# Reading turned attention probabilities back from the DRAM scratch in two halves instead of one transfer

## The chip, the core and the metric

The kernel runs on one core of one Trainium2 chip. The metric is the device time of one launch in microseconds (us). A lower number is better.

## What is computed

The reference is one decoder block over 512 positions with 1024 channels (the Griffin-style merge of a gated short convolution and of native sparse attention, then a feed-forward part with a short convolution). Cut to what matters here:

```python
proj = rmsnorm(x, norm1_g) @ w_in            # split into a_b, a_c, a_x, q, k/v of three branches, gates
y_a = a_b * causal_dwconv(a_c * a_x, conv_a_w)
# per head group g and block of 128 queries, for the selected and for the window branch:
s = einsum('bqghd,bkgd->bghqk', qc, k) * scale
p = masked_softmax(s, mask)                  # over the keys
o = einsum('bghqk,bkgd->bqghd', p, v)
y_b = gate0 * o_cmp + gate1 * o_sel + gate2 * o_win
mix = sigmoid(gA) * (y_a @ w_a_out) + sigmoid(gB) * (y_b @ w_b_out)
x = x + mix @ w_o
x = x + (silu(causal_dwconv(g) + b) * u) @ w_ffn_out      # g, u = split(rmsnorm(x) @ w_ffn_in)
```

With 512 positions and 8 key blocks of 64 all blocks are selected, so that both the selected and the window branch see every key up to the query.

## The kernel before

Matrix products are computed from pairs of values, a rounded part and its remainder (`h` and `l` in names), so that each product of two tiles takes three matmuls. All matmuls run on TensorE (PE). In order of time: the token-wise projections, then (from about 98 us to 295 us) the attention, then the output projection and the feed-forward part.

**Attention.** `attend` (line 609) is called for each tile of 128 queries, `qt` = 3, 2, 1, 0, and each of two head groups `g`. A tile `qt` sees `qt + 1` tiles of 128 keys. For `qt` > 0 each call makes two steps, one for the window branch (`br` = 1) and one for the selected branch (`br` = 0); for `qt` = 0 both branches make one step. I call such a step a *turn*, since its centre is the function `turn` (line 624): turn 1 is `qt` 3, `g` 0, `br` 1; turn 2 is `br` 0 of it; turns 3 and 4 are the same with `g` 1; turns 5 to 8 belong to `qt` 2, 9 to 12 to `qt` 1, 13 and 14 to `qt` 0. There are fourteen, and only turns 1 to 4 have four key tiles.

One turn goes like this. PE makes the scores of four heads into PSUM banks (lines 640 and 641). VectorE (DVE) adds the causal mask and takes the maximum (692, 693). ScalarE (ACT) takes the exponentials (694) and scales them by the sums and gates (700). The probabilities then lie with queries on the partitions, while the product with the values needs keys there. `turn` does that in three parts: DVE transposes in blocks of 32 by 32 (627); four transfers on SyncE's queue (SP) write the blocks to a scratch in DRAM (633); one transfer reads them back with the keys on the partitions, into a tile `tn` (635). Per key tile `kt`, ACT copies the rounded part `ph` (724), GpSimd (POOL) subtracts it from `tn` to leave the remainder (725), and PE multiplies both by the values into the bank `po` (727 and 732). Of `ph` there are two buffers (`NPT`), and of `tn` two (`NTN`), so that the read-back of a turn waits until PE has used up the turn two before it.

**What lies beside it.** The products of the short convolution (`pa`, line 762) and of the merge gates (`pg`, 783; `pma`, 796) don't depend on the attention and fill PE between its steps. Each takes a weight tile: loaded on SP into one of three `wr` buffers (139), rounded by ACT (143), and its remainder taken by POOL (145; in conv tiles partly by a DMA). A weight load can be issued only when POOL has finished with the tile three loads earlier. All of these stand in SP's one queue together with the turns' transfers.

**What sets the order.** Nothing is ordered by hand around the change. The program is built with a scheduler (`schedule_with_timeline_sim=True`, line 1143), which places the instructions of every engine by its own estimates of their times. Each engine then works through its list in order on the chip, waiting where a semaphore isn't there yet.

Of the kernel before, what the change touches and what calls it, by code (L numbers as in the profile page):

```python
# [22 lines left out]
NT = S // P  # L23
# [30 lines left out]
QB = P // SQ  # L54
# [31 lines left out]
def tile_block(ctx: ExitStack, tc: tile.TileContext, xT, pos, par, par2, w_tok, w_a3, w_gate, w_ao, w_bo, w_o,  # L86
               w_ff, w_dn, c_w1, out):
    nc = tc.nc
# [90 lines left out]
    def ring_w(src, name):  # L179
        raw = raw_tile(name)  # L180
        nc.sync.dma_start(raw, src)
        h, l = ring(name)
        split(h, l, raw)
        return h, l
# [424 lines left out]
    def attend(pt_, g, qt):  # L609
# [14 lines left out]
        def turn(e, n):  # L624

            v = e.rearrange("p b k h i -> p (b k h i)")
            nc.vector.transpose(v, v)
            w = n * P
            dst = pt_.tile([P, HG * S], F32R, name=f"tn_{e.name}", tag="tn", bufs=NTN)[:, 0:QB * w]
            d = dst.bitcast(F32)  # L630
            mid = dr.tile([QB, QB, SQ, w], F32, name=f"td_{e.name}", tag=f"td_{e.name}", bufs=1)
            for a in range(QB):
                nc.sync.dma_start(mid[a].rearrange("b j r -> j b r"),
                                  v[a * SQ:(a + 1) * SQ].rearrange("p (b r) -> p b r", b=QB))
            nc.sync.dma_start(d.rearrange("p (a r) -> p a r", a=QB), mid.rearrange("a b j r -> (b j) a r"))
            return dst.rearrange("p (a k r) -> p a k r", a=QB, k=n)

        def scores(w, i, br, a, b):
# [18 lines left out]
        if qt == 0:  # L657

            e = e_tile("", 2)
            mx = pt_.tile([P, HG, 2], F32, name=f"mx{tag}", tag="mx", bufs=1)  # L660
            sums = small("sums", 2)
            for i in range(HG):
                sc = s_bank(f"sc{tag}{i}")
                w = sc[:, 0:2 * (NC + P)].rearrange("p (b k) -> p b k", b=2)
                for j in range(2):
                    nc.tensor.matmul(w, q[:, g * HG + i, :], kk5[:, j, :, g, 0:NC + P], start=j == 0, stop=j == 1)
                nc.vector.tensor_add(xc[:, i, :], w[:, 0, 0:NC], cm_add[:, qt, :])
                dg = w[:, :, NC:]
                nc.vector.tensor_tensor(dg, dg, causal[:, None, :].to_broadcast([P, 2, P]), op=ALU.add)
                nc.vector.tensor_reduce(mx[:, i], dg, axis=AX.X, op=ALU.max, negate=True)  # L670
                for br in (1, 0):
                    nc.scalar.activation(e[:, :, br, i], dg[:, br].rearrange("p (b i) -> p b i", i=SQ), AF.Exp,
                                         bias=mx[:, i, br:br + 1], accum_out=sums[:, i, br:br + 1])
            nc.vector.reciprocal(sums, sums)
            nc.gpsimd.tensor_mul(sums, sums, gates[:, :, 1:3])
            for br in (1, 0):
                nc.vector.tensor_tensor(e[:, :, br], e[:, :, br],
                                        sums[:, None, :, br:br + 1].to_broadcast([P, QB, HG, SQ]), op=ALU.mult)
            turned = turn(e, 2)
        for br in (1, 0):  # L680
            if qt > 0:
                o = off if br == 0 else 0
                e = e_tile(br, qt + 1)
                mx = small(f"mx{br}", 1)
                sums = small(f"sums{br}", 1)
                for i in range(HG):
                    sc = s_bank(f"sc{tag}{i}{br}")
                    scores(sc[:, 0:o + nk], i, br, NC - o, NC + nk)
                    if o:
                        nc.vector.tensor_add(xc[:, i, :], sc[:, 0:NC], cm_add[:, qt, :])  # L690
                    dg = sc[:, o + nk - P:o + nk]
                    nc.vector.tensor_add(dg, dg, causal)
                    nc.vector.tensor_reduce(mx[:, i], sc[:, o:o + nk], axis=AX.X, op=ALU.max, negate=True)
                    nc.scalar.activation(e[:, :, :, i].rearrange("p b k i -> p k b i"),
                                         sc[:, o:o + nk].rearrange("p (k b i) -> p k b i", b=QB, i=SQ), AF.Exp,
                                         bias=mx[:, i], accum_out=sums[:, i])
                scale_of(sums, 1 + br)
                for i in range(HG):
                    v = e[:, :, :, i]
                    nc.scalar.activation(v, v, AF.Copy, scale=sums[:, i])  # L700
                turned = turn(e, qt + 1)
# [18 lines left out]
            for kt in range(qt + 1):  # L720
# [5 lines left out]
                w = v_t[:, kt, 2 * br + g, :]  # L726
# [116 lines left out]
    for i in range(4):  # L843
# [3 lines left out]
        w = ring_w(w_bo[i], f"bo{i}")  # L847
# [33 lines left out]
    for n, j in enumerate(O_ORDER):  # L881
        w = ring_w(w_o[j], f"o{j}")
# [265 lines left out]
```

## Time and profile before

| what | before |
|---|---|
| time, median of 3 runs | 700.33 us (699.7 to 702.07) |
| the profiled execution | 700.2 us, of which span 698.5 us |
| PE busy | 690.7 us (99% of the span) |
| ACT, DVE, POOL busy | 436.8, 508.3, 242.6 us |
| DMA, mean over the span | 179 GB/s |
| HBM read, written | 111.55 MB, 12.58 MB |

The profiled execution is 0.13 us below the median. The span is the time from its first to its last instruction; 1.7 us lie around it. Matmuls are pipelined: one of 512 columns is listed with about 0.39 us, but in an unbroken row the next one starts 0.227 us after it. So a wait of PE is read from the distance between starts.

### The profile page before, as it was taken

The numbers are of one execution on the slowest core, as the hardware profiler recorded it, in microseconds if no ns is written. First come the engines' busy times: TensorE is split into PE (matmuls) and PEld (weight loads), VectorE is DVE, ScalarE is ACT, GpSimd is POOL, SyncE is SP. The second block draws the span as 40 slices with busy tenths as digits, with TensorE's granted clock in tenths as the row PEclk, the third lists the DMA queues.
The fourth block names the chain that finished last, engine by engine and source line by source line (L and its number), as shares of the span: only waits on it lengthen the run. The fifth ranks groups of instructions, "written<-read, shape, count | busy, mean of one in ns | idle before, by whom it ended". The sixth has DMA issues, their size and how long they took to land.

```text
span 698.5 us, 11286 instructions
## 1 busy us (share of the span) xinstructions
PE 690.7 (99%) x4125; PEld 616.7 (88%) x4125; DVE 508.3 (73%) x886; ACT 436.8 (63%) x775; POOL 242.6 (35%) x240
## 2 busy tenths in 40 slices
PE   9999999999999999999999999999999999999997
PEld 8999878887888888888889999999999999999986
DVE  6886885766576646475887899988787777877543
ACT  7634654777897877534685777766466665556530
POOL 3060423476887867452011212121112221112110
PEclk9999999999999999999999999999999999999999
DMA  7333586577676555563486797997977879775675
GB/s 272 108 96 122 156 184 143 139 254 216 230 232 224 164 174 148 186 237 117 135 194 127 196 230 175 239 201 183 228 180 167 210 178 221 180 177 108 129 141 150
DMA packets 56167, 124.87 MB, mean 179 GB/s; under 512 B 5040, under 2 KB 20528, under 8 KB 56112
## 3 DMA queue, kind: packets, MB, share of 16 engines
q1 hardware_dynamic: 41984, 91.39, 40.8%
q0 software_dynamic: 13840, 32.51, 27.1%
q8 instruction: 32, 0.52, 0.3%
q10 hardware_dynamic: 288, 0.26, 0.1%
q14 instruction: 23, 0.19, 0.1%
HBM read 111.55 MB, written 12.58 MB: 178 GB/s over the span
## 4 chain that ended last, share of the span: by engine, by line
PE 89%; DMA 5%; ACT 2%; DVE 1%; issue 1%; SPq 0%; ACTq 0%
PE p L418 10%; PE p L417 10%; PE p L420 10%; PE pdn L418 6%; PE pdn L417 6%; PE pdn L420 6%; PE pg L417 4%; PE pg L418 4%; PE pg L420 4%; PE po L418 2%; PE po L417 2%; PE po L420 2%; DMA tn_e<-td_e 2%; PE pa L417 2%; PE pa L418 2%; PE pj_s L264 2%
## 5 line engine op out<-in xcount | busy, mean ns | idle before, releaser
L418 PE MATMUL p<-xf_l,sh 128*128 128x256 f32 x336 | 80.6, 277 | 0.0
L417 PE MATMUL p<-xf_h,sh 128*128 128x256 f32 x336 | 80.5, 277 | 0.0
L170 POOL DMA_DIRECT2D wl_s<-in_w_ff_dram x22 | 19.4, 883 | 167.2 <-ACT wl_s L169 146.4
L162 ACT ACTIVATE sh<-s 128x1024 fp32r<-128x1024 f32 x44 | 46.2, 1057 | 37.4 <-PE p L418 24.7
L418 PE MATMUL pdn<-al,wh_d 128*128 128x512 f32 x176 | 68.7, 391 | 0.0
L417 PE MATMUL pdn<-ah,wh_d 128*128 128x512 f32 x176 | 68.5, 390 | 0.0
L417 PEld LDWEIGHTS p<-xf_h,sh 128*128 128x128 f32 x336 | 63.0, 188 | 0.1
L418 PEld LDWEIGHTS p<-xf_l,sh 128*128 128x128 f32 x336 | 63.0, 188 | 0.1
L163 DVE TENSOR_TENSOR sl<-s,sh 128x1024 fp32r<-128x1024 f32 x44 | 53.6, 1220 | 8.7 <-ACT sh L162 8.7
L725 POOL TENSOR_TENSOR tn_e<-tn_e,ph 128x512 fp32r<-128x512 f32 x40 | 51.2, 1296 | 16.0 <-ACT ph L724 15.9
L168 ACT ACTIVATE wh_s<-wr_s 128x1024 fp32r<-128x1024 f32 x22 | 23.3, 1059 | 53.3 <-PE pdn L418 50.1
L170 POOL DMA_DIRECT2D wl_d<-in_w_dn_dram x22 | 26.4, 1199 | 76.5 <-ACT wl_d L169 69.2
L420 PE MATMUL p<-xf_h,sl 128*128 128x256 f32 x336 | 51.5, 277 | 0.0
L417 PE MATMUL pg<-xg_h,wh_g 128*128 128x512 f32 x128 | 50.1, 392 | 0.0
L418 PE MATMUL pg<-xg_l,wh_g 128*128 128x512 f32 x128 | 50.1, 392 | 0.0
L420 PE MATMUL pdn<-ah,wl_d 128*128 128x512 f32 x176 | 47.7, 389 | 0.0
L420 PEld LDWEIGHTS p<-xf_h,sl 128*128 128x128 f32 x336 | 44.5, 188 | 0.2
L1067 DVE TENSOR_TENSOR x<-x,pdn 128x512 f32<-128x512 f32 x48 | 32.9, 685 | 16.2 <-PE pdn L420 15.5
L145 POOL TENSOR_TENSOR wl_g<-wr_g,wh_g 128x1024 fp32r<-128x1024 f32 x16 | 38.5, 2408 | 10.0 <-ACT wh_g L143 9.7
L417 PE MATMUL p<-xf_h,wh_s 128*128 128x256 f32 x168 | 40.5, 276 | 0.0
L418 PE MATMUL p<-xf_l,wh_s 128*128 128x256 f32 x168 | 40.5, 276 | 0.0
L420 PEld LDWEIGHTS pdn<-ah,wl_d 128*128 128x128 f32 x176 | 33.0, 188 | 6.9
(358 smaller groups left out, 2095.6 us busy)
## 6 DMA issues: line engine op xcount, KB each, us to landing
wr_s<-in_w_ff_dram SPq DMA_DIRECT2D x44, 512.0 KB, 5.2
wl_s<-in_w_ff_dram POOLq DMA_DIRECT2D x22, 512.0 KB, 7.5
wr_d<-in_w_dn_dram SPq DMA_DIRECT2D x22, 512.0 KB, 6.8
wl_d<-in_w_dn_dram POOLq DMA_DIRECT2D x22, 512.0 KB, 8.7
wr_g<-in_w_gate_dram SPq DMA_DIRECT2D x16, 512.0 KB, 4.5
wr_a<-in_w_a_dram SPq DMA_DIRECT2D x12, 512.0 KB, 3.5
tl<-in_w_ff_dram POOLq DMA_DIRECT2D x22, 256.0 KB, 7.6
td_e<-e SPq DMA_DIRECT2D x16, 256.0 KB, 4.7
```

What stands on the lines that cost most here:

```text
L145: e.tensor_sub(lo[:, 0:n], raw[:, 0:n], hi[:, 0:n].bitcast(F32))
L162: hi = nc.scalar.activation(h, v, AF.Copy)
L163: nc.vector.tensor_sub(l, v, h.bitcast(F32))
L168: nc.scalar.activation(h, raw, AF.Copy)
L170: nc.gpsimd.dma_start(l if dst is None else dst, src, accum_op=ALU.add)
L264: nc.tensor.matmul(acc, xg_h[:, k, ts_], wh, start=k == 0, stop=False)
L417: nc.tensor.matmul(acc, wh, xh, start=first and i == 0, stop=False)
L418: nc.tensor.matmul(acc, wh, xl, start=False, stop=False)
L420: nc.tensor.matmul(acc, wl, xh, start=False, stop=last and i == len(units) - 1)
L725: nc.gpsimd.tensor_sub(pl, pt, ph.bitcast(F32))
L1067: nc.vector.tensor_add(xj, xj, acc)
```

## The change

The read-back of a turn with four key tiles (`n == NT`) becomes two transfers. The first brings the columns of key tiles 0 and 1 of every block, the second those of key tiles 2 and 3. Turns with two or three key tiles keep one transfer. The bytes are the same; the rows that a transfer reads from the scratch have 1024 bytes instead of 2048.

```diff
-            nc.sync.dma_start(d.rearrange("p (a r) -> p a r", a=QB), mid.rearrange("a b j r -> (b j) a r"))
+            back, from_ = d.rearrange("p (a r) -> p a r", a=QB), mid.rearrange("a b j r -> (b j) a r")
+            for c in ((slice(0, w // 2), slice(w // 2, w)) if n == NT else (slice(0, w),)):
+                nc.sync.dma_start(back[:, :, c], from_[:, :, c])
             return dst.rearrange("p (a k r) -> p a k r", a=QB, k=n)
```

From here on a line of the changed kernel has a number higher by 2 (635 becomes 637, 724 becomes 726, 727 becomes 729). In the built program the copies of key tiles 0 and 1 wait for the first transfer alone, those of key tiles 2 and 3 for the second.

The scheduler lays the attention out anew. Up to the read-back of turn 1 the lists of all five engines are the same, and from the end of the attention on they are the same again. Every engine but SP has the same instructions as before, in another order; SP has four transfers more.

The first place is PE at the first use of turn 1 (the rows of `po_1020`; `ph_1062` is the rounded part of key tile 0, and `pa` and `pg` are filling products). Before:

```order
L418 MATMUL pa_2455<-xg_l,wh_a_2450 128x512
L417 MATMUL pa_2455<-xg_h,wh_a_2450 128x512
L418 MATMUL pa_2455<-xg_l,wh_a_2450 128x512
L420 MATMUL pa_2455<-xg_h,wl_a_2451 128x512 x8
L727 MATMUL po_1020<-ph_1062,v_t 128x512
L417 MATMUL pg_2490<-xg_h,wh_g_2485 128x512
```

The same place of the changed kernel, where `ph_1063` is that key tile:

```order
L418 MATMUL pa_2459<-xg_l,wh_a_2454 128x512
L417 MATMUL pa_2459<-xg_h,wh_a_2454 128x512
L418 MATMUL pa_2459<-xg_l,wh_a_2454 128x512
L420 MATMUL pa_2459<-xg_h,wl_a_2455 128x512 x2
L729 MATMUL po_1020<-ph_1063,v_t 128x512
L420 MATMUL pa_2459<-xg_h,wl_a_2455 128x512 x6
L417 MATMUL pg_2494<-xg_h,wh_g_2489 128x512
```

The first use of turn 1 has moved six matmuls ahead.

The second place is PE at the first use of turn 3 (`po_1177`, `ph_1219`). Before:

```order
L420 MATMUL pma_2571<-y_1002,wl_ao_2553 128x512 x4
L640 MATMUL sc_1387<-kk,qT_791 128x416
L641 MATMUL sc_1387<-kk,qT_791 128x416
L727 MATMUL po_1020<-ph_1157,v_t 128x512
L640 MATMUL sc_1394<-kk,qT_791 128x416
L641 MATMUL sc_1394<-kk,qT_791 128x416
L727 MATMUL po_1177<-ph_1219,v_t 128x512
L732 MATMUL po_1020<-tn_e_1082_1116,v_t 128x512
```

The same place of the changed kernel (`po_1179`, `ph_1222`):

```order
L643 MATMUL sc_1398<-kk,qT_791 128x416
L417 MATMUL pg_2596<-xg_h,wh_g_2591 128x512
L418 MATMUL pg_2596<-xg_l,wh_g_2591 128x512
L417 MATMUL pg_2596<-xg_h,wh_g_2591 128x512
L418 MATMUL pg_2596<-xg_l,wh_g_2591 128x512
L417 MATMUL pg_2596<-xg_h,wh_g_2591 128x512
L418 MATMUL pg_2596<-xg_l,wh_g_2591 128x512
L729 MATMUL po_1179<-ph_1222,v_t 128x512
L734 MATMUL po_1020<-tn_e_1083_1117,v_t 128x512
```

Six filling matmuls now stand right ahead of it. Counted from the matmul at which the two orders part, turn 3 is first used after 117 matmuls before and after 123 now; turn 5 after 253 before and 223 now; turn 7 after 338 and 316; turn 11 after 504 and 503.

The third place is SP's queue from turn 1's read-back to turn 5's (`tn` is a read-back, `td` the four writes of a turn; `e_1178` and `e_1180` are turn 3, `e_1239` and `e_1242` turn 4). Before:

```order
L635 DMA tn_e_1021_1055<-td_e_1021_1056 128x4x512
L633 DMA td_e_1082_1117<-e_1082 32x4x512 x4
L139 DMA wr_g_2586<-in_w_gate_dram 128x1024
L635 DMA tn_e_1082_1116<-td_e_1082_1117 128x4x512
L139 DMA wr_g_2620<-in_w_gate_dram 128x1024
L633 DMA td_e_1178_1213<-e_1178 32x4x512 x4
L139 DMA wr_ao_2653<-in_w_ao_dram 128x1024
L635 DMA tn_e_1178_1212<-td_e_1178_1213 128x4x512
L139 DMA wr_g_2688<-in_w_gate_dram 128x1024
L633 DMA td_e_1239_1274<-e_1239 32x4x512 x4
L635 DMA tn_e_1239_1273<-td_e_1239_1274 128x4x512
```

The changed kernel:

```order
L637 DMA tn_e_1021_1055<-td_e_1021_1056 128x4x256 x2
L633 DMA td_e_1083_1118<-e_1083 32x4x512 x4
L139 DMA wr_g_2590<-in_w_gate_dram 128x1024
L637 DMA tn_e_1083_1117<-td_e_1083_1118 128x4x256 x2
L139 DMA wr_g_2624<-in_w_gate_dram 128x1024
L139 DMA wr_ao_2657<-in_w_ao_dram 128x1024
L633 DMA td_e_1180_1215<-e_1180 32x4x512 x4
L637 DMA tn_e_1180_1214<-td_e_1180_1215 128x4x256 x2
L633 DMA td_e_1242_1277<-e_1242 32x4x512 x4
L139 DMA wr_g_2692<-in_w_gate_dram 128x1024
L139 DMA wr_g_2726<-in_w_gate_dram 128x1024
L637 DMA tn_e_1242_1276<-td_e_1242_1277 128x4x256 x2
```

The load of the weight tile `wr_ao` has moved ahead of turn 3's writes, and two loads of `wr_g` ahead of turn 4's read-back.

## The prediction

> **What bounds the kernel now.** I read the page first, then PE's waits, then the starts of its matmuls around them, then the chain of waits. The page:
>
> ```profile
> PE 690.7 (99%) x4125; PEld 616.7 (88%) x4125; DVE 508.3 (73%) x886; ACT 436.8 (63%) x775; POOL 242.6 (35%) x240
> ```
>
> PE is at work nearly all the time, and the change takes no matmul away. All that it can win is time in which PE waits. In the stretch that the change re-orders, 120 to 300 us, PE's waits are one row (total, times, longest):
>
> ```profile
> PE po L727 <- ACT ph L724: 1.8, 2, 1.7
> ```
>
> Both are first uses of a turn: turn 1 and turn 3. PE's own rows there (start, duration, idle before in brackets):
>
> ```profile
> 144.57 1.98 PE L420 MATMUL pa<-xg_h,wl_a 128*128 128x512 f32 x8
> 146.71 0.50 PE L727 MATMUL po<-ph,v_t 128*128 128x512 f32 x1 [0.16 <-ACT ph L724]
> 147.04 0.39 PE L417 MATMUL pg<-xg_h,wh_g 128*128 128x512 f32 x1
> ...
> 170.95 0.35 PE L641 MATMUL sc<-kk,qT 128*128 128x416 f32 x1
> 172.97 0.50 PE L727 MATMUL po<-ph,v_t 128*128 128x512 f32 x1 [1.67 <-ACT ph L724]
> 173.31 0.40 PE L732 MATMUL po<-tn_e,v_t 128*128 128x512 f32 x1
> ```
>
> The listed idle is too small, since durations overlap; I count starts. Eight matmuls from 144.57 at 0.227 us end at 146.39, so turn 1's use at 146.71 is 0.32 late, and the next start comes 0.33 instead of 0.23 later: 0.43 lost. At turn 3 the score matmul of 416 columns takes 0.19 (416/512 of 0.227), so 171.14 was possible and 172.97 came, with 0.11 again behind it: 1.94. Together **2.37 us**, the most that can go. About 0.3%, here 2.1 us, is what a measurement of this kernel can tell from no change, so even the full prize is just visible.
>
> The chain of waits says what these two uses waited for (start, duration, what):
>
> ```profile
> 134.44 5.23 DMA td_e<-e
> ...
> 139.76 6.24 DMA tn_e<-td_e
> ...
> 160.40 4.58 DMA td_e<-e
> ...
> 165.03 7.15 DMA tn_e<-td_e
> ```
>
> The last write to the scratch, then the read-back of 1 MB, at turn 1 and again at turn 3. The read-back is the step that the change cuts.
>
> **The change part by part.** What half a read-back costs needn't be guessed: turns with two key tiles read exactly such transfers, 512 KB in rows of 1024 bytes. From the DMA issues (count, size, median us to landing), and below them the fastest and the slowest of those reads:
>
> ```profile
> tn_e<-td_e SPq DMA_DIRECT2D x4, 1024.0 KB, 6.1
> ...
> tn_e<-td_e SPq DMA_DIRECT2D x6, 512.0 KB, 4.1
> ```
> ```profile
> tn_e<-td_e SPq DMA_DIRECT2D x1, 512.0 KB, 3.8
> tn_e<-td_e SPq DMA_DIRECT2D x1, 512.0 KB, 4.8
> ```
>
> So the first half should land after 4.1 us (3.8 to 4.8) instead of 6.1: 2.0 us sooner. [...]
>
> The second half. Its rows are shorter, so I compare what the queue's packets cost in a window that holds one 512 KB read (256.3 to 260.3 us) and one that holds a 1 MB read (148.5 to 154.4 us):
>
> ```profile
> q1 hardware_dynamic: 528, 0.52, 43.1%
> ```
> ```profile
> q1 hardware_dynamic: 612, 1.33, 70.5%
> ```
>
> 43.1% of 16 engines for 4.0 us are 27.6 engine-us for 0.52 MB, or 18.8 KB per engine-us; 70.5% for 5.9 us are 66.6 for 1.33 MB, or 20.0. Short rows cost 6% more, on the 3.3 us that 1 MB takes on 16 engines 0.2 us. With 0.43 us for one more issue (SP's rows below: 0.38 and a gap) the second half lands at most 0.6 us later than the whole did. Nobody feels it: in turn 1 it would land by 146.6, and the use of the third key tile stands 30 matmuls (6.8 us) behind that of the first. [...]
>
> SP. Four issues more. In turn 1 the writes of turn 2 follow:
>
> ```profile
> 139.76 0.38 SPq L635 DMA_DIRECT2D tn_e<-td_e  x1
> 141.29 0.31 SPq L633 DMA_DIRECT2D td_e<-e  x1
> ```
>
> They were issued 1.5 us after the read-back, when DVE had transposed, so that 0.43 for one more issue is hidden there; without that cover turn 2 would start 0.43 later.
>
> Turn 1. The first half lands at 139.76 + 4.1 = 143.9 (143.6 to 144.6). From landing to PE's use it was 0.7 us (146.00 to 146.71), so 144.6 (144.3 to 145.3). The use now stands six matmuls earlier, at 144.57 + 2 × 0.227 = 145.0. Wait gone, or 0.3 left at worst.
>
> Turn 3. Its first use stands six matmuls later in the list (117 before, 123 now). Without waits PE came there at 171.14 - 0.43 = 170.7; now at 170.7 + 6 × 0.227 = 172.1. When is the data there? These rows of ACT, POOL and SP carry the answer:
>
> ```profile
> 146.02 1.15 ACT L724 ACTIVATE ph<-tn_e 128x512 fp32r<-128x512 f32 x2 [4.51 <-DMA tn_e<-td_e]
> ...
> 153.90 2.56 ACT L700 ACTIVATE e<-e,sums 128x512 f32<-128x512 f32 x4
> 156.36 0.29 ACT L711 ACTIVATE xs<-xc 128x128 fp32r<-128x128 f32 x1
> 156.56 0.67 ACT L694 ACTIVATE e<-sc,mx 128x512 f32<-128x512 f32 x1
> ...
> 157.22 1.05 ACT L143 ACTIVATE wh_ao<-wr_ao 128x1024 fp32r<-128x1024 f32 x1
> ```
> ```profile
> 158.35 2.42 POOL L145 TENSOR_TENSOR wl_ao<-wr_ao,wh_ao 128x1024 fp32r<-128x1024 f32 x1 [1.16 <-ACT wh_ao L143]
> ```
> ```profile
> 158.83 2.87 SPq L633 DMA_DIRECT2D td_e<-e  x4
> 161.74 1.21 SPq L139 DMA_DIRECT2D wr_ao<-in_w_ao_dram  x1
> ```
>
> ACT stood idle for 4.51 us until the read-back of turn 1 and goes on 2.1 us sooner. But ahead of turn 3's scaling (L700) its new list has four instructions that stood behind it: an exponential of turn 4, a rounding copy of turn 2, the weight copy `wh_ao` and the small copy `xs`, 0.67 + 0.63 + 1.05 + 0.3 = 2.6 us. So the scaling starts at 153.9 - 2.1 + 2.6 = 154.4, 0.5 later. From its start to the first write it was 158.83 - 153.90 = 4.93, to the last landing of the writes 164.98 - 158.83 = 6.15 more (160.40 + 4.58), then 4.1 for half a read and 0.7: 154.4 + 4.93 + 6.15 + 4.1 + 0.7 = 170.3 (170.0 to 171.0). PE comes at 172.1. Wait gone, with 1.8 us to spare (1.1 to 2.1).
>
> On SP the load of `wr_ao` now stands ahead of these writes, and it waits until POOL has finished `wl_ao` of the load three before: at 158.35 + 2.42 = 160.77 in this trace, while the writes want to go at 154.4 + 4.93 = 159.3. POOL waited there for ACT's copy, which comes about 4 us earlier (157.22 to 153), so I take the load as hidden; without that cover the writes go 1.5 us later, which the spare 1.8 just holds.
>
> What is late next. The scheduler now uses turns 4 to 10 much earlier: turn 5 after 223 matmuls instead of 253, turn 7 after 316 instead of 338. At turn 5 the trace shows ACT's rounding copy and PE's use:
>
> ```profile
> 198.34 0.63 ACT L724 ACTIVATE ph<-tn_e 128x512 fp32r<-128x512 f32 x1
> ```
> ```profile
> 202.83 0.39 PE L727 MATMUL po<-ph,v_t 128*128 128x512 f32 x1
> ```
>
> Without the two waits PE came there at 200.5, and 30 matmuls (6.6 us, a few of them short) earlier is 193.8. If turn 5's data came no sooner than before (198.97), PE would wait 5.2 us; if it keeps up with the plan, 0. Both ends are open, since the whole chain of exponentials, writes and reads moves with the plan. How wrong can a plan of this scheduler be? In this trace two of fourteen first uses were planned too early, by 0.43 and 1.94 us. I take one such place, at their mean, **1.2 us**; the bounds are 0 and 5.2.
>
> **The sum.** For the profiled execution 700.2 - 2.37 + 1.2 = 699.0; its time is 0.13 us under the median, so 700.33 - 2.37 + 1.2 = **699.2 us**.
>
> **The rivals.**
>
> *The whole prize* (chance 0.18). Both waits go and none comes: 700.33 - 2.37 = 698.0. For it: ends 0 above, spare time at turns 1 and 3. Against: turns 4 to 10 lose the reserve they had.
>
> *Only moved* (0.20). The load of `wr_ao`, now right ahead of turn 3's writes, is not hidden and shares the DMA engines with them; the spare 1.8 goes, and turn 3 or one behind it waits: 1.7 to 3 us in all, so 699.7 to 701.0, no change. For it: reads of the same size differ by a microsecond with what lies beside them, 7.15 at turn 3 and 6.24 at turn 1.
>
> *Slower* (0.12): turn 5 isn't ready. SP's list holds two loads of `wr_g` ahead of turn 4's read-back, each waiting for POOL's 2.4 us subtraction, and turn 5's writes stand behind that read. If POOL is late there, turns 4 and 5 keep their old times while PE comes 6.6 us earlier. At the full 5.2 us: 700.33 - 2.37 + 5.2 = 703.2. It decides against the change when turn 5's copy is ready after 193.8 + 4.5 = 198.3 us, about when it was before. Against it: the reads of turns 1, 3 and 4 can all start or land sooner than before, and ACT has its idle time before them to give.
>
> *The change doesn't do what it says*, if both halves had to land before the first copy: excluded, as the built program lets key tiles 0 and 1 wait for the first transfer alone.
>
> **How the numbers follow.** The forecast has 0.50, the rivals 0.18, 0.20 and 0.12. Faster by over 0.3% (below 698.2) is the whole prize, 0.18; slower by over 0.3% (above 702.4) is the last, 0.12; the rest, 0.70, is within 0.3%. The range of 697.9 to 702.0 leaves out the slower case (0.12) and somewhat under half of the whole prize, which a measurement can put on either side of 698.0 (0.08).
>
> **What would show it.** In the changed kernel's trace: the first halves land 3.8 to 4.8 us after issue; turn 1's first use without idle before it, near 145.0; turn 3's writes issued near 159.3 and its use near 172 without a wait; PE's waits between 120 and 300 us in rows at turns 4 to 10, together about 1.2 us by starts. The prediction is wrong if turn 3 still waits over 1 us, or if a turn behind it waits over 3; then the spare time of the new plan is what failed.

## The result, and the profile after

The changed kernel is slower: 705.82 us (median of 6 runs, 704.38 to 706.58) beside 701.2 us for the kernel before (6 runs, the three above among them, 699.03 to 702.22). The ratio is 1.0071, with a 95% interval of 1.0056 to 1.0085: 5.0 us, 3.9 to 6.0. The forecast was 699.2 us, no change, in a range that ended at 702.0. The profiled execution took 706.34 us, of which span 704.6 us.

PE's waits in the same stretch, 120 to 300 us (total, times, longest):

```profile
PE po L729 <- ACT ph L726: 3.7, 5, 1.9
```

Before there were two such waits, 1.8 us in all, both at turns 1 and 3. Counted by the starts of matmuls, as in the prediction, PE loses 8.6 us in this stretch and lost 3.3 before (small steps at many matmuls included). Where it does so is seen from PE's busy time by stretches (stretch, its length, busy time and instructions of PE, its weight loads, DVE, ACT and POOL, granted clock, DMA share, GB/s). Before:

```profile
160.00:180.00 20.00, 18.33 (x84) 15.09 (x83) 12.77 (x28) 15.86 (x35) 14.76 (x12) 1.00 0.79 220
220.00:240.00 20.00, 20.00 (x95) 16.75 (x95) 10.69 (x33) 17.15 (x48) 18.53 (x17) 1.00 0.68 207
280.00:300.00 20.00, 20.00 (x92) 16.52 (x92) 8.28 (x12) 10.56 (x15) 9.05 (x7) 1.00 0.62 202
```

After:

```profile
160.00:180.00 20.00, 19.95 (x90) 16.48 (x89) 10.34 (x24) 14.57 (x33) 12.36 (x10) 1.00 0.79 247
220.00:240.00 20.00, 18.13 (x88) 14.95 (x88) 10.05 (x29) 15.18 (x43) 15.56 (x14) 1.00 0.65 183
280.00:300.00 20.00, 18.77 (x83) 14.73 (x82) 6.80 (x10) 10.39 (x15) 11.82 (x9) 1.00 0.51 163
```

The hole at 160 to 180 (turn 3) is filled, as meant. Two new ones have opened, at 220 to 240 (turn 8) and at 280 to 300 (turn 14). Neither turn has anything to do with the read-backs that were cut. By starts the waits of the new kernel are 0.3 us at turn 3, 0.4 at turn 4 and 0.3 at its last key tile, 0.3 at turn 6, 0.7 at turn 7, **2.1 at turn 8**, 0.8 at turn 10, 0.5 at turn 12, 0.8 at turn 13, 0.4 at a transposition, and **1.45 at turn 14**.

At turn 1 the change does what it says. PE's rows there:

```profile
143.98 0.62 PE L420 MATMUL pa<-xg_h,wl_a 128*128 128x512 f32 x2
144.44 0.39 PE L729 MATMUL po<-ph,v_t 128*128 128x512 f32 x1
```

144.44 less 0.45 for two matmuls is 143.98: no wait. Turn 8 is the opposite. Its read-back and first use, from the chain of waits of the changed kernel (start, duration, what):

```profile
218.84 6.61 DMA tn_e<-td_e
225.53 0.64 ACT ph L726
226.21 0.50 PE po L729
```

and how long PE waited, from its own row:

```profile
226.21 0.50 PE L729 MATMUL po<-ph,v_t 128*128 128x512 f32 x1 [1.87 <-ACT ph L726]
```

In the kernel before, turn 8's read-back was issued at 219.97 and PE's first use stood at 229.00:

```profile
219.97 0.38 SPq L635 DMA_DIRECT2D tn_e<-td_e  x1
```
```profile
tn_e<-td_e SPq DMA_DIRECT2D x1, 768.0 KB, 5.2
```
```profile
229.00 0.39 PE L727 MATMUL po<-ph,v_t 128*128 128x512 f32 x1
```

It landed at 219.97 + 5.2 = 225.1, and at 218.84 + 6.61 = 225.45 in the changed kernel: the data comes no sooner. But PE, which used it at 229.00 before, now asks for it at 224.2 (226.21 less the 2.0 us that it waits by starts), and would have asked earlier still without the waits ahead.

### The profile page after: what moved, and what is told of

The parts are those of the page before. It is cut to its first block, busy times and chain, and to the rows that moved or that the text cites. A ratio compares the mean times of both kernels' runs of the same rounds, so it can differ in the third digit from the quotient of the medians.

```text
span 704.6 us, 11289 instructions
## 1 busy us (share of the span) xinstructions
PE 695.2 (99%) x4125; PEld 616.8 (88%) x4125; DVE 511.3 (73%) x886; ACT 436.4 (62%) x775; POOL 245.1 (35%) x240
## 4 chain that ended last, share of the span: by engine, by line
PE 84%; DMA 7%; ACT 2%; DVE 2%; POOL 2%; issue 1%; SPq 1%; ACTq 0%; DVEq 0%; POOLq 0%
PE p L418 10%; PE p L417 10%; PE p L420 10%; PE pdn L418 6%; PE pdn L417 6%; PE pdn L420 6%; DMA tn_e<-td_e 4%; PE pa L420 3%; PE pa L417 3%; PE pa L418 3%; DMA td_e<-e 2%; PE po L418 2%; PE po L420 2%; PE po L417 2%; PE pj_s L264 2%; PE pj_s L266 2%
## 5 line engine op out<-in xcount | busy, mean ns | idle before, releaser
L627 DVE STREAM_TRANSPOSE e<-e 128x1024 f32<-128x1024 f32 (+2 forms) x14 | 23.8, 1701 | 23.7 <-ACT e L702 22.7
```

## The experiments

The theory after reading the two traces: the cut transfers do what was forecast of them, and the loss is the new **order**, whose plan for turns 5 to 14 is earlier than the data can be (order theory). The rival: the **transfers** themselves cost it, by shorter rows, four more issues, and fuller DMA engines (transfer theory).

To tell these apart, an order can be held. A table holds, for each engine, the sequence in which its instructions stood in one of the two built programs, and neighbours in it are tied without a semaphore, so that the scheduler has nothing left to choose there:

```diff
+        ops = [by[e][k] for k in at]
+        for a, b in zip(ops, ops[1:]):
+            tc.add_manual_dep(b, a.name, mybir.DependencyInfo(mybir.DependencyClass.NoSync, mybir.DependencyReason.DATA),
+                              reason="order")
...
         tile_block(tc, **args)
+        lay(nc, tc)
```

Times below are medians; the ratio is to the kernel before on the same chip, with its 95% interval.

### Two transfers, the order of before

The changed kernel, with the table of before for all five engines.

> The changed kernel with its two transfers, but every engine's list held to the order of the kernel before (SP's with the second half right behind the first). Order theory (the new lists plan turns 5 to 14 too early; the two transfers gain what was forecast): the waits at turns 1 and 3 go (2.37 us by starts), nothing takes their place, turns 8 and 14 don't wait: about 2.4 us under the kernel before, 698 to 700. Transfer theory (shorter rows, four more issues and more crowded engines slow the turns whatever the order): as slow as the changed kernel, 4 to 5 us over the kernel before, with PE waiting at turns 8 and 14 again.

699.59 us (11 runs), ratio 0.9987 (0.9978 to 0.9995): 0.9 us under the kernel before. PE's waits from 120 to 300 us:

```profile
PE po L729 <- ACT ph L726: 0.5, 1, 0.5
PE po L734 <- POOL tn_e L727: 0.2, 1, 0.2
```

The sign is the order theory's, and the transfer theory is out by more than 4 us. The size isn't as expected. The waits at turns 1 and 3 are gone (2.37 us), but by starts about 0.9 us came back at the last key tiles of turn 4 and 0.8 at turn 13. That part was only moved.

### One transfer, the order of the changed kernel

The kernel before, with the table of the changed one.

> The kernel before with its one transfer, but every engine's list held to the order of the changed kernel. Order theory: as slow as the changed kernel or slower; turn 1 and turn 3 are now used by a plan that counts on halves, so turn 1 waits about 1.8 us (six matmuls, 1.36, more than its 0.43) and turn 3 about 2; behind them PE is late anyway, which takes about as much off the waits of turns 8 and 14: 705 to 710 us, 4 to 8 over the kernel before. Transfer theory: within 1 us of the kernel before.

707.19 us (5 runs), ratio 1.0098 (1.0085 to 1.0112): 6.9 us over. PE's waits:

```profile
PE po L727 <- ACT ph L724: 5.5, 6, 1.7
```

By starts 0.9 us at turn 1, 2.0 at turn 3, 1.8 at turn 8, 1.2 at turn 14. This gives the whole square (us against the kernel before, worked out from the ratios):

| | order of before | order of the changed kernel |
|---|---|---|
| one transfer | 0 | +6.9 (6.0 to 7.8) |
| two transfers | -0.9 (-1.5 to -0.4) | +5.0 (3.9 to 6.0) |

The order costs 6 to 7 us with either form of transfer. The two transfers win 1 to 2 us with either order.

### The halves the other way round

```diff
-            for c in ((slice(0, w // 2), slice(w // 2, w)) if n == NT else (slice(0, w),)):
+            for c in ((slice(w // 2, w), slice(0, w // 2)) if n == NT else (slice(0, w),)):
```

> The halves in the other order: key tiles 2 and 3 come first, 0 and 1 second, so that the first use of a turn waits for both. PE, ACT, DVE and POOL have word for word the order of the kernel before, and so has SP but for the four additional transfers. Order theory: the kernel before, plus at most 0.6 us later landing at each of turns 1 and 3: 0 to 1.2 us over it. Transfer theory: 4 to 5 us over it.

701.88 us (12 runs), ratio 1.0017 (1.0005 to 1.0028): 1.2 us over, the upper end of what the order theory gave. All the extra transfers are here, a turn's first use waits for both halves, and yet it isn't 4 to 5 us. Part of the 1.2 comes with PE's clock: in the profiled execution eight matmuls behind turn 3's wait ran at half pace, 1.5 us (below, on the hardware), and the five of the 12 runs with a mean granted clock below 0.999 took 701.93 to 703.78 us, the other seven 700.42 to 701.89.

### Two transfers in turns 1 and 2 alone

```diff
-            for c in ((slice(0, w // 2), slice(w // 2, w)) if n == NT else (slice(0, w),)):
+            for c in ((slice(0, w // 2), slice(w // 2, w)) if n == NT and g == 0 else (slice(0, w),)):
```

> Two transfers in turns 1 and 2 alone, whole reads in turns 3 and 4. The scheduler's lists differ from those of the kernel before only up to the first use of turn 5 and are the same from there on; turn 3 is first used after 128 matmuls (117 before, 123 in the changed kernel), turn 5 after 253 as before. Order theory: turn 1's wait goes, turn 3's shrinks or goes, since it is planned 2.5 us later than before; turns 8 and 14 don't wait: 1.5 to 2.4 us under the kernel before. Transfer theory: half of the extra transfers, half of the loss, about 2.5 us over it.

701.13 us (11 runs), ratio 1.0005 (0.9995 to 1.0014): no change; neither theory had that. Turn 3 didn't lose its wait:

```profile
174.77 0.50 PE L729 MATMUL po<-ph,v_t 128*128 128x512 f32 x1 [1.40 <-ACT ph L726]
```

PE was planned 2.5 us later there, but the data came later as well: SP issued turn 3's writes at 160.84 (158.83 before), as soon as DVE had transposed (158.50 + 2.31), and the whole read-back landed at 174.0 instead of 172.2. So an earlier start of turns 1 and 2 isn't passed on to turn 3. What the run does show is that turns 8 and 14, back at their old places, have no wait of note (0.6 us at most by starts).

### The first key tile of turns 5 to 8 by itself

```diff
-            for c in ((slice(0, w // 2), slice(w // 2, w)) if n == NT else (slice(0, w),)):
+            for c in ((slice(0, w // 2), slice(w // 2, w)) if n == NT else (slice(0, P), slice(P, w)) if n > 2 else (slice(0, w),)):
```

> The changed kernel with one thing more: in the turns with three key tiles (5 to 8) the first key tile comes in a transfer of its own, ahead of the other two. All five engines' lists are those of the changed kernel word for word but for SP's four transfers. If the waits behind the changed plan are data that lands too late for it, the first tile lands about 2 us sooner there, and the waits at the first uses of turns 5 to 8 (by starts 0.3 + 0.3 + 0.7 + 2.1 = 3.4 us) go, while turn 14's 1.45 stays: 702 to 703 us, 2.7 to 3.4 under the changed kernel. If PE waits there for something else (ACT's own list, POOL), or each wait only moves to the next turn, it stays within 1 us of the changed kernel.

702.34 us (7 runs), ratio 1.0023 (1.0009 to 1.0038), 3.4 us under the changed kernel by the ratios. Between 190 and 225 us three of these first tiles are read, and the rest of them behind (count, size, median us to landing); below them the four undivided reads of the changed kernel:

```profile
tn_e<-td_e SPq DMA_DIRECT2D x3, 512.0 KB, 5.0
tn_e<-td_e SPq DMA_DIRECT2D x3, 256.0 KB, 3.6
```
```profile
tn_e<-td_e SPq DMA_DIRECT2D x4, 768.0 KB, 5.5
```

The same plan, met with data that lands 1.9 us sooner, waits that much less: turn 8's 2.1 us are gone (0.5 is left at turn 7) and turn 14's wait stays (1.1 by starts). More transfers made it faster, which the transfer theory can't have.

### PE's list alone

The changed kernel, with PE's new table and the old ones for ACT, DVE, POOL and SP.

> Two transfers as in the changed kernel, PE's list of the changed kernel, but ACT, DVE, POOL and SP held to their lists of before. If PE's early plan is the cause, PE waits from turn 5 on for copies that ACT makes as late as before (turn 5: ACT at about 198, PE at 194): 5 us or more over the kernel before, as slow as the changed kernel or slower. If it is the other engines' new lists that make the data late (ACT's copies and exponentials in a worse order), it is within 2 us of the kernel before, and turn 14 doesn't wait.

751.94 us (5 runs), ratio 1.0744 (1.072 to 1.0769): 52 us over. The direction is as expected of an early plan, but nobody had expected a size like this, so it doesn't measure the plan. PE's list and the others' are fitted to each other, and each engine works through its own in order; PE waits 21 times in these four rows, on ACT and on POOL:

```profile
PE po L729 <- ACT ph L726: 17.8, 10, 3.8
PE po L734 <- POOL tn_e L727: 9.6, 7, 2.7
PE ptc L717 <- POOL xs L714: 3.8, 2, 2.1
PE sc L668 <- ACT e L674: 3.8, 2, 2.0
```

PE's clock, at 0.98 of full speed in the mean of these runs, has its part in the 52 us too. With PE's new list the other four are needed, so that going back with them doesn't show whether they have a cost of their own. At turn 14 they have one, which is shown next.

### Turn 14 ahead of turn 13's copies

In the changed kernel's chain, turn 13's read-back is followed by turn 14's last exponentials (line 674), although DVE had taken the last maximum for them by 269.7:

```profile
269.33 0.41 DVE L672 TENSOR_REDUCE mx<-sc 128x2 f32<-128x256 f32 x1
```

```profile
269.84 3.83 DMA tn_e<-td_e
...
274.30 0.61 ACT ph L726
...
274.94 0.59 ACT yt L736
275.53 0.92 ACT xc L709 x6
276.46 0.03 ACT e L674
...
276.72 0.55 ACT e L674 x3
```

On ACT's list turn 13's two copies stand ahead of these two exponentials, and ACT waits for the read-back in front of them. In the kernel before, ACT took the two exponentials at 270.54 and 270.88, before turn 13's read-back had landed (275.31), and turn 14's writes went 6 us sooner:

```profile
274.73 1.76 SPq L633 DMA_DIRECT2D td_e<-e  x4
```

The edit, on ACT's list (DVE's reciprocal of the sums, and POOL's product with the gates, move ahead in the same way):

```diff
+L674 ACTIVATE e,sums<-sc,mx 128x4x32 x2
 L726 ACTIVATE ph<-tn_e 128x512
 L726 ACTIVATE ph<-tn_e 128x512
 L736 ACTIVATE yt<-po 64x512
-L709 ACTIVATE xc,mcs<-xc,mcs 128x32 x3
-L674 ACTIVATE e,sums<-sc,mx 128x4x32 x2
-L709 ACTIVATE xc,mcs<-xc,mcs 128x32
+L709 ACTIVATE xc,mcs<-xc,mcs 128x32 x4
```

> The changed kernel with one place of its lists mended: turn 14's last two exponentials on ACT stand ahead of turn 13's copies (behind them in the changed kernel, so that ACT waited 3.3 us for turn 13's read-back with turn 14's exponentials ready to go), and DVE's and POOL's steps of turn 14 that follow from them stand ahead of what waits for turn 13. If that queue is what makes turn 14 late, its data comes about 5 us sooner and the wait of 1.45 us by starts goes: 1.2 to 1.8 us under the changed kernel, 704 to 704.6. If turn 14 is late for another reason (its scores, the transfers), no change.

703.26 us (5 runs, 702.96 to 705.29), ratio 1.0051 (1.0036 to 1.0065): 1.4 us under the changed kernel by the ratios. In the profiled execution, the slowest of the five, turn 14's writes went at 280.06 instead of 280.68 and 0.97 us of its wait were left: the mending was half done. DVE's scaling of turn 14 (679) still stood behind a reciprocal (646) that waits for ACT's work behind those copies. The next one moves that too:

```diff
 L676 RECIPROCAL sums<-sums 128x8
-L786 TENSOR_TENSOR t_all<-pg,rb_n 128x512
-L646 RECIPROCAL mcs<-mcs 128x4
 L679 TENSOR_TENSOR e<-e,sums 128x4x128 x2
 L627 STREAM_TRANSPOSE e<-e 128x1024
+L786 TENSOR_TENSOR t_all<-pg,rb_n 128x512
 L739 TENSOR_TENSOR yo<-po,yt 64x256 x2
+L646 RECIPROCAL mcs<-mcs 128x4
```

> The changed kernel with turn 14 mended as before and one step more: DVE's reciprocal of the compressed branch, which waits for ACT work behind turn 13's copies, now stands behind turn 14's scaling and transposition instead of ahead of them (in the mending before, turn 14's scaling still stood behind it and started at 277.4 with its sums ready at 272.1). If that queue is the cause, turn 14's writes go at about 276 instead of 280.7, its data lands by 284 and its wait (0.86 by starts was left) goes: 0.5 to 1.3 us under the first mending, 702 to 702.8. If not, as slow as that.

702.71 us (8 runs), ratio 1.003 (1.002 to 1.004): 2.9 us under the changed kernel, 1.5 under the half mending. SP's rows show turn 14's writes, in the changed kernel

```profile
280.68 1.94 SPq L633 DMA_DIRECT2D td_e<-e  x4
```

and here

```profile
273.17 1.94 SPq L633 DMA_DIRECT2D td_e<-e  x4
```

7.5 us sooner, by the places of a few instructions in three lists, and PE's wait at turn 14 is gone. Not all of the gain is turn 14's: between the two profiled executions 1.7 us of the difference lie at turns 3 to 10 (turn 8 waits 1.5 us by starts, 2.1 in the changed kernel), ahead of anything that the edit touches.

### Both mendings

> Both mendings of the changed plan together: the first key tile of turns 5 to 8 in its own transfer, and turn 14's steps ahead of turn 13's copies. PE's list is still the changed kernel's word for word. If the loss is these waits and no cost of the transfers or of the order as such, the two gains add (3.5 us and 1 to 2 us): 700 to 701.5, within 0.1% of the kernel before. If a cost is left that has to do with neither, it stays at 702 or more.

700.93 us (11 runs), ratio 1.0004 (0.9995 to 1.0013). The loss of 5.0 us is gone, with PE's list still that of the changed kernel word for word, and no wait of PE is listed between 120 and 300 us (0.5 us at most by starts, 2.8 in the whole stretch, where the kernel before loses 3.3). The gains don't add in full: apart they were 3.4 and 2.9 us, together 4.7, as part of the second wasn't turn 14's. To within the interval, the loss was these waits and nothing else.

### From the other side: mending the order of before

The first run left 0.9 us at turn 4 and 0.8 at turn 13. First attempt: PE's uses there put one to four matmuls further back, at turn 4 like this (at turn 13 the first use goes behind four filling matmuls):

```diff
 L729 MATMUL po<-ph,v_t 128x512
-L734 MATMUL po<-tn_e,v_t 128x512
-L729 MATMUL po<-ph,v_t 128x512
 L642 MATMUL sc<-kk,qT 128x416
 L643 MATMUL sc<-kk,qT 128x416
-L734 MATMUL po<-tn_e,v_t 128x512
 L417 MATMUL pg<-xg_h,wh_g 128x512
+L418 MATMUL pg<-xg_l,wh_g 128x512
+L734 MATMUL po<-tn_e,v_t 128x512
+L729 MATMUL po<-ph,v_t 128x512
...
+L734 MATMUL po<-tn_e,v_t 128x512
```

> The best candidate: two transfers with all lists of the kernel before, and two places of PE's list mended where that version still waited: turn 4's last three uses stand one to four matmuls further back, turn 13's first use four matmuls further back. Those waits were 0.48 + 0.11 + 0.16 + 0.11 us and 0.67 + 0.11 by starts. If PE's lateness there was only a matter of place, they go and nothing else comes: 1.2 to 1.6 us under the version without the mending, 698 to 698.6, 0.3% or more under the kernel before. If the time is lost to the next turn instead, it is as slow as that version, 0.1% under the kernel before.

699.92 us (11 runs), ratio 0.9989 (0.9978 to 1.0001): nothing won. Turn 13's wait went; turn 4's came back at the very next matmul:

```profile
194.64 0.46 PE L642 MATMUL sc<-kk,qT 128*128 128x416 f32 x1 [0.92 <-ACT e L696]
```

This is a score matmul, and it waits for ACT too. So ACT was late, and PE only met it at another place. Why ACT was late stands in its own waits of the first run, between 180 and 190 us, with the transfers that it waited for:

```profile
ACT e L696 <- DMA td_e<-e: 3.6, 1, 3.6
```
```profile
td_e<-e SPq DMA_DIRECT2D x4, 192.0 KB, 7.0
```

Turn 5's writes took 7.0 us, beside the second half of turn 4's read-back and a load of `wr_g` issued just ahead of them; ACT's exponentials of the turn after next need their buffer back. The second attempt puts that load behind the writes in SP's queue, and keeps PE's edit at turn 13 alone:

```diff
 L637 DMA tn_e<-td_e 128x4x256 x2
-L139 DMA wr_g<-in_w_gate_dram 128x1024
 L633 DMA td_e<-e 32x4x384 x4
+L139 DMA wr_g<-in_w_gate_dram 128x1024
```

> Best candidate: two transfers with the lists of the kernel before, mended at two places. SP issues turn 5's writes ahead of the load of wr_g that stood between turn 4's read-back and them (they landed 7 us after issue, and ACT's exponentials waited 3.6 us for them to give the buffer back, which made turn 4's last uses 0.86 us late); PE's first use of turn 13 stands four matmuls further back (0.78 late). If those are the two causes: 1.2 to 1.7 us under the version without the mending, 698 to 698.5, 0.3% or more under the kernel before. If the wait at turn 4 is not made by the writes, only turn 13's part: 0.8 under.

698.4 us (5 runs, 697.91 to 699.05), ratio 0.997 (0.9958 to 0.9982): 2.1 us under the kernel before, the fastest of all. The same two rows:

```profile
ACT e L696 <- DMA td_e<-e: 1.0, 1, 1.0
```
```profile
td_e<-e SPq DMA_DIRECT2D x4, 192.0 KB, 5.2
```

1.8 us off the writes, 2.6 off ACT's wait, and the full prize of the prediction, 2.37 us, is nearly all there.

### Two transfers in turns 3 and 4 alone

```diff
-            for c in ((slice(0, w // 2), slice(w // 2, w)) if n == NT else (slice(0, w),)):
+            for c in ((slice(0, w // 2), slice(w // 2, w)) if n == NT and g == 1 else (slice(0, w),)):
```

> Two transfers in turns 3 and 4 alone, nothing ordered by hand: the scheduler leaves the lists of PE, ACT, DVE and POOL as they were before. Order theory: turn 3's 1.9 us go, turn 1's 0.43 stays, and some comes back at turn 4 and turn 13 as in the version with all halves and the old order: 0.5 to 1.4 us under the kernel before. Transfer theory: 2 us or more over it.

700.45 us (12 runs), ratio 0.9997 (0.9988 to 1.0006). The scheduler leaves the four lists alone, and the loss doesn't come. No gain is seen either: in the profile turn 3's wait shrinks to 0.3 us, but turn 1 waits 0.8 us (0.43 before), and 1.4 us come back at turn 13, 0.8 at turn 4. That is a little worse than I expected (the interval reaches 0.8 us under the kernel before), and the same moving as in the first run.

## Why the prediction was wrong

**What bounds the kernel, and the prize: right.** PE's waits were worth 2.37 us, and the best version won 2.1 (1.3 to 2.9).

**The first half: about right at turns 1 to 3, wrong at turn 4.** It was to land after 4.1 us (3.8 to 4.8). From the DMA issues of the changed kernel, turn 1's and turn 4's first halves:

```profile
tn_e<-td_e SPq DMA_DIRECT2D x1, 512.0 KB, 3.5
```
```profile
tn_e<-td_e SPq DMA_DIRECT2D x1, 512.0 KB, 6.9
```

Turns 2 and 3 took 4.5 and 3.6. Turn 4's was read while two loads of `wr_g` came in, and took longer than the whole read before (5.9). At turn 1 half of 1 MB saved 6.24 - 3.5 = 2.7 us, where 2.0 was forecast.

**The second half: wrong, in both directions.** It was to land up to 0.6 us later than the whole. Counted from the first issue it landed after 5.4, 5.9, 5.7 and 8.4 us at turns 1 to 4, while the whole took 6.2, 5.8, 7.2 and 5.9: sooner at turns 1 and 3, the same at turn 2, and 2.5 us later at turn 4, beside the loads. The 6% for short rows, worked out from packets in two windows, isn't seen as a delay at turns 1 to 3. The reversed halves agree: PE had no wait at turn 1 although its first use there needs both.

**Turn 1 and turn 3: right, the spare time of turn 3 wasn't.** Turn 1's wait went. Turn 3's went from 1.94 to 0.33 by starts, where 1.8 us to spare had been worked out. Rows of ACT, DVE and SP show where they went:

```profile
155.34 2.55 ACT L702 ACTIVATE e<-e,sums 128x512 f32<-128x512 f32 x4
157.93 2.31 DVE L627 STREAM_TRANSPOSE e<-e 128x2048 f32<-128x2048 f32 x1 [1.77 <-ACT e L702]
159.44 0.35 SPq L139 DMA_DIRECT2D wr_ao<-in_w_ao_dram  x1
160.26 2.75 SPq L633 DMA_DIRECT2D td_e<-e  x4
167.32 0.93 SPq L637 DMA_DIRECT2D tn_e<-td_e  x2
```

ACT's scaling was to start at 154.4 and started at 155.34, as ACT had waited 1.45 us for a maximum of DVE shortly before (at 153.00). The writes followed when DVE had transposed (157.93 + 2.31 = 160.24). The load of `wr_ao` had been issued by 159.8 and didn't hold them up, so that the cover which the prediction took was there. But the writes took 6.92 us to the last landing (167.18) instead of 6.15, beside the load: in the seven runs with the load ahead of these writes they take 6.5 to 7.0 us, in the seven with the load behind them 6.1 to 6.2. The half read was 0.5 us faster than forecast, and PE came 0.6 us sooner, at 171.5.

**The term that failed: "one place planned too early by mean 1.2 us".** It was to stand for all of turns 4 to 14; by starts PE lost 7.7 us there, at eight turns and one transposition. None was over 3 us, the mark at which the prediction would have given its theory up: many waits below a mark add up as well as one above it. The order and the rows of the trace before held most of the answer. For one place, turn 5, the prediction compared the new plan with the old data, and there it read the wrong row: ACT's copy at 198.34 has no wait in brackets, and turn 5's read-back had landed 5.4 us before it. The copy only stood late in ACT's list; in the changed kernel it came at 192.88. PE used turn 5 at 193.91 without a wait, so that the rival "slower", given 0.12, had the sign right and the place wrong; nor did the two loads of `wr_g` hold up turn 4's read-back, which was issued 0.15 us after the last of its writes had landed (175.98 and 175.83). What should have been compared is, for every turn, the landing in the trace before with PE's new place. PE's use before, less the landing, is the spare time; a copy takes 0.7 of it, the new plan takes 0.227 for every matmul that the first use has moved ahead, and the two waits that go take 2.37:

| turn | read-back landed, before | first use, before | spare | matmuls moved ahead | short by |
|---|---|---|---|---|---|
| 5 | 192.97 | 202.83 | 9.9 | 30 (6.8 us) | 0.0 |
| 6 | 203.78 | 211.82 | 8.0 | 26 (5.9 us) | 0.9 |
| 7 | 216.50 | 220.29 | 3.8 | 22 (5.0 us) | 4.3 |
| 8 | 225.14 | 229.00 | 3.9 | 19 (4.3 us) | 3.5 |
| 10 | 242.04 | 246.93 | 4.9 | 26 (5.9 us) | 4.1 |
| 13 | 275.31 | 276.54 | 1.2 | 22 (5.0 us) | 6.8 |
| 14 | 282.35 | 283.40 | 1.1 | -4 (-0.9 us) | 1.1 |

"Short by" is how far behind its plan PE would be at that turn, in all, if the data landed when it did before; it needn't be added up. From turn 4 on PE had in fact lost 3.8 us by turn 8, 4.6 by turn 10 and 5.9 by turn 13, where the table says 3.5, 4.1 and 6.8. Turn 5, the one place that was looked at, is one without a loss. Two rows don't fit. At turn 7 PE had lost 1.7 us and not 4.3, as the read-back landed 2.6 us sooner than before (213.87). At turn 14 it was 7.7 and not 1.1: PE's place there is no earlier than before, but the read-back landed 6.3 us later (288.61), behind the two exponentials that had moved in ACT's list. So the new order cost time in two ways: PE's uses were planned ahead of the data, up to turn 13, and ACT's list made the data late, at turn 14. The table finds only the first.

**Why the data comes no sooner.** The prediction left open whether turns 5 to 14 would move with the plan. Taken together they didn't. Turn 8's scaling on ACT, before and after:

```profile
209.81 2.12 ACT L700 ACTIVATE e<-e,sums 128x384 f32<-128x384 f32 x4
```
```profile
209.79 2.14 ACT L702 ACTIVATE e<-e,sums 128x384 f32<-128x384 f32 x4
```

19 matmuls of plan, and 0.02 us of difference. ACT works its list in order, and what it waits for between 140 and 260 us is the scratch, in the changed kernel more than before:

```profile
ACT ph L724 <- DMA tn_e<-td_e: 10.0, 4, 4.5
ACT e L694 <- DMA td_e<-e: 4.2, 3, 2.3
```
```profile
ACT ph L726 <- DMA tn_e<-td_e: 12.5, 8, 3.6
ACT e L696 <- DMA td_e<-e: 4.9, 4, 1.8
```

The exponentials of one turn stand behind the copies of an earlier one, which wait for its read-back, and they need a buffer that is free only when an earlier turn's writes have landed. From turn 6's landing to turn 8's it is 21.4 us before and 21.7 after. Turns 5, 6, 8 and 10 landed within 0.3 us of their old times; turns 7, 9 and 13 came 1.6 to 2.6 us sooner, turns 11, 12 and 14 2.2 to 6.3 us later. So the landings don't follow PE's places, and the loop of ACT and the scratch is what fits as their pace.

**Still only argued:** why the scheduler's plan is so early. Its estimates of the transfers may be shorter than what the chip shows, but no run measured them. That the loop of ACT and the scratch sets the pace is argued too; no run loosened it alone.

## What to carry to other kernels

Where a scheduler lays out the order, an edit is two changes, and the second can be the bigger one: here -0.9 us for the transfers and +6 us for the order they brought along. Before such an edit is judged, hold the old order or compare, for every consumer and not for the first one, the time at which its data landed with its new place, and look in the producers' lists for work that now stands behind a wait. A wait that has been cured in one place is first looked for where the same engine next meets the same producer; here it went only when the producer was relieved (turn 5's writes took 7.0 us beside a load that had time, and 5.2 ahead of it).

## What the hardware showed beside that

PE's clock fell to about half behind waits, but not behind all. In the run with the halves reversed, PE waited 0.3 and 1.6 us by starts within 2.5 us, and the matmuls from 172.87 to 176.23 came 0.43 apart instead of 0.227. Its windows (clock in the third column from the end):

```profile
173.00:176.50 3.50, 3.50 (x11) 2.74 (x10) 2.87 (x8) 3.45 (x7) 3.10 (x4) 0.55 0.72 190
176.50:180.00 3.50, 3.50 (x17) 2.96 (x16) 2.89 (x6) 3.42 (x8) 2.54 (x2) 1.00 0.67 219
```

With PE's list alone changed the same followed a wait listed with 3.8 us:

```profile
203.00:206.50 3.50, 3.50 (x11) 2.83 (x11) 1.05 (x3) 1.92 (x6) 2.17 (x2) 0.58 0.32 77
```

In both places it took 3.4 us until the matmuls came at their full pace again (172.87 to 176.23 and 202.63 to 206.00), about 1.5 us lost. From 218.2 to 223.0 us of the run with PE's list alone changed it stood at 0.50 for the whole 4.8 us. The changed kernel's wait of 2.0 us at turn 8 and the kernel before's of 1.8 at turn 3 had no such price (clock 1.00 in 3.5 us behind each, from 226.5 and from 173.0). The clock fell here behind waits of 0.3 and 1.6 us, and in another place not behind one of 2.0, so that its price can't be read from a wait's length alone. What makes it fall was not shown.
